# Down projection: the even rows of the raw weights and the rows of x are issued behind the odd rows of the fourth tile

## The chip, the cores and the metric

The kernel runs on one core of a Trainium2 chip. The metric is the device time of one execution in microseconds, the median of three runs: 2437.94 (2428.3 to 2442.87). The profile is of one further execution, which took 2436.62 with a span of 2434.6.

## The reference, cut to what matters

The reference is an encoder of two post-norm layers over a sequence of 1024 rows of 1024 float32 values. Each layer has a token mixer (a convolution group, a differential attention group and an attention over 256 memory rows) and then a channel mixer:

```python
for l in range(DEPTH):
    mixed = hybrid_mixer(x, mem, bias_off, ...)
    x = layer_norm(ALPHA * x + mixed, ln1_g[l], ln1_b[l])
    ff = jnp.square(jax.nn.relu(x @ w_up[l])) @ w_down[l]
    x = layer_norm(ALPHA * x + ff, ln2_g[l], ln2_b[l])
```

`w_up` is 1024 x 4096, `w_down` is 4096 x 1024. The change lies in the product with `w_down`, once in each layer.

## The kernel before

A float32 product is made of three products of halves: every operand is split into a high part, rounded to the matmul's type, and the low part that is left (`split`, lines 96 to 102: ScalarE writes the high part, VectorE the low one). On top of that both products of the channel mixer use a seven-product scheme for 2 x 2 blocks (Strassen's, in Winograd's form): seven block products in place of eight, on sums and differences of blocks.

The up projection goes over 16 pairs of hidden tiles. For each pair it writes seven forms of the hidden values to DRAM (`hd`, `keep`, line 928), since the down projection wants them as its stationary operands.

The down projection (lines 997 to 1152) has two groups `gr` of weight rows, and in each the seven products in the order `PRODS = (3, 1, 5, 6, 2, 7, 4)`. One product is 96 matmuls of 512 columns: four tiles `q`, four row blocks `t`, six matmuls each (two halves of the contraction by three products of halves). A tile `q` of the raw weights, `wd`, is 128 x 4 x 1024: four row groups of 512 KB, each its own DMA from SyncE's queue (`down_raw`, line 1020). `place` (line 1003) says which block a product takes. Product 3, the first, takes block (1, 1), which lies in the odd row groups 1 and 3. Product 1, the second, takes block (0, 0), which lies in the even row groups 0 and 2. From product 5 on the blocks are differences that VectorE makes in place (lines 1034 to 1039), and they need both.

`down_forms` (lines 1028 to 1053) makes one tile's operands for one product: the differences, the split weights `wf` (128 x 1024), the load of the hidden forms `hr` (two DMAs of 256 KB from `hd`, lines 1049 and 1050) and their split `hf`. The raw tiles of the first group lie in slots of the pool tag `b16`, which hold the transposed x of the up projection until its last readers are done. The fourth tile, `wd_0_3`, gets the slot whose last reader is the last matmul group of the up projection (`uc`, line 905).

What sets the order: the Tile framework schedules each engine's instructions from a model of times and allocates the slots. `tc.issue_after(ins)` adds the condition that what the block issues on the engine of `ins` stands behind `ins`. In the kernel before, the even rows of the four tiles and the rows of x for the first four blocks (`yd`, `down_rows`, line 1058) stand behind `loads[-1]`, which is there the last load of hidden forms for product 3, tile 3. That load is early on SyncE's queue, since its pairs are done early.

In names as the instruction order prints them, `wd_0_3` is group 0, tile 3; `wf_0_1_2` and `hf_0_1_2` are group 0, product 1, tile 2; the last number is a buffer's. The profile leaves numbers out: `db` and `dz` are the accumulators of the down projection (`db` of product 3, `dz` of product 1 in the first group).

Of the kernel before, what the change touches and what calls it, by code (L numbers as in the profile page):

```python
# [54 lines left out]
def encoder(ctx: ExitStack, tc: tile.TileContext, x, memt, w_f, w_v, w_mk, w_mv, w_out, w_up,  # L55
# [40 lines left out]
    def split(hi, lo, src, lo_eng=None, hi_eng=None):  # L96

        if hi_eng is None:
            nc.scalar.activation(hi, src, AF.Copy)  # L99
        else:  # L100
            hi_eng.tensor_scalar(hi, src, 1.0, 0.0, ALU.mult, ALU.add)
        (lo_eng or nc.vector).tensor_tensor(lo, src, f(hi), op=ALU.subtract)  # L102

    loads = []
# [661 lines left out]
    for l in range(L):  # L766
# [230 lines left out]
        with ExitStack() as es:  # L997
# [12 lines left out]
            def down_raw(gr, q, rows=(0, 1, 2, 3)):  # L1010

                if (gr, q) not in wr:
                    if gr and q < 2:
                        r = pd.tile([P, 4, 1024], F32, tag="wd", name=f"wd{l}_{gr}_{q}", bufs=2)
                    else:
                        r = big.tile([P, 4, 1024], F32, tag="b16", name=f"wd{l}_{gr}_{q}", bufs=4)
                    wr[gr, q] = r.rearrange("p (b i) (j d) -> p b i j d", b=2, j=2)
                m0 = 4 * (NQ * gr + q)
                for i in rows:
                    loads.append(nc.sync.dma_start(wr[gr, q][:, i // 2, i % 2].rearrange("p j d -> p (j d)"), w_down[l, (m0 + i) * P:(m0 + i + 1) * P, :]))  # L1020

            def form_tile(tag, name, q):

                if q == 3:
                    return wts.tile([P, 2, 2, 512], F32R, tag="w8", name=name, bufs=3)
                return pd.tile([P, 2, 2, 512], F32R, tag=tag, name=name, bufs=3)

            def down_forms(gr, i, q):

                r = wr[gr, q]  # L1030
                v = {k: r[:, :, k[0], k[1]] for k in ((0, 0), (0, 1), (1, 0), (1, 1))}
                tt = nc.vector.tensor_tensor
                if i == 5:
                    tt(v[0, 0], v[0, 1], v[0, 0], op=ALU.subtract)
                    tt(v[0, 1], v[1, 1], v[0, 1], op=ALU.subtract)
                elif i == 6:
                    tt(v[1, 1], v[1, 1], v[0, 0], op=ALU.subtract)
                elif i == 4:
                    tt(v[1, 0], v[1, 1], v[1, 0], op=ALU.subtract)
                if not gr and i == PRODS[0] and q < 2:  # L1040

                    w = [big.tile([P, 2, 512], F32R, tag="y4", name=f"wf{l}_{gr}_{i}_{q}_{n}", bufs=8) for n in range(2)]
                else:
                    w = form_tile("wf", f"wf{l}_{gr}_{i}_{q}", q)
                    w = [w[:, 0], w[:, 1]]
                split(w[0], w[1], v[place[i]])
                hr = wts.tile([P, 2, 512], F32, tag="raw", name=f"hr{l}_{gr}_{i}_{q}", bufs=3)
                p0 = 2 * (NQ * gr + q)
                for n in range(2):
                    loads.append(nc.sync.dma_start(hr[:, n], hd[p0 + n][:, form_of[i]]))  # L1050
                h = form_tile("hf", f"hf{l}_{gr}_{i}_{q}", 3 if not gr and i == PRODS[0] and q < 2 else q)
                split(h[:, 0], h[:, 1], hr)
                return w, h

            def down_rows(ts):
                for t in ts:
                    ys[t] = ytile(f"yd{l}_{t}")
                    nc.sync.dma_start(ys[t], xmid[l][t])
# [44 lines left out]
            cur = []  # L1103
            for q in range(NQ):
                down_raw(0, q, (1, 3))
                cur.append(down_forms(0, PRODS[0], q))

            with tc.issue_after(loads[-1].ins):
                for q in range(NQ):
                    down_raw(0, q, (0, 2))  # L1110
                down_rows(range(4))
# [113 lines left out]
def build(arrays):  # L1225
    import concourse.bacc as bacc

    nc = bacc.Bacc("TRN2", target_bir_lowering=False, num_devices=1, dynamic_dma_scratch_size=1024)
    args = [nc.dram_tensor(f"in_{k}", v.shape, mybir.dt.from_np(v.dtype), kind="ExternalInput").ap() for k, v in arrays.items()]
    args.append(nc.dram_tensor("out_0", (T, D), F32, kind="ExternalOutput").ap())  # L1230
    with tile.TileContext(nc, schedule_with_timeline_sim=True) as tc:
        encoder(tc, *args)
    return nc
# [9 lines left out]
```

## Time and profile before

| | before |
|---|---|
| median of 3 runs | 2437.94 us (2428.3 to 2442.87) |
| profiled execution | 2436.62 us, span 2434.6 us |
| TensorE busy | 2322.3 us (95%), 11516 matmuls |
| VectorE busy | 1770.3 us (73%) |
| ScalarE busy | 1176.0 us (48%) |
| SyncE's DMA queue | 353.81 MB, 43.1% of 16 engines |

The span starts with the first instruction of the program. The chain that ended last lies on TensorE for 77% of the span, so a stretch in which TensorE stands still is where time can go or come from. The shares of the DMA queue are means over stages: in some stretches the queue is full all the time, in others nearly empty, so a stretch has to be read by itself. The first layer's down projection begins at about 912 us, the second's at about 2097 us.

### The profile page before, as it was taken

The numbers are of one execution on the slowest core, as the hardware profiler recorded it, in microseconds if no ns is written. First come the engines' busy times: TensorE is split into PE (matmuls) and PEld (weight loads), VectorE is DVE, ScalarE is ACT, GpSimd is POOL, SyncE is SP. The second block draws the span as 40 slices with busy tenths as digits, with TensorE's granted clock in tenths as the row PEclk, the third lists the DMA queues.
The fourth block names the chain that finished last, engine by engine and source line by source line (L and its number), as shares of the span: only waits on it lengthen the run. The fifth ranks groups of instructions, "written<-read, shape, count | busy, mean of one in ns | idle before, by whom it ended". The sixth has DMA issues, their size and how long they took to land.

```text
span 2434.6 us, 30636 instructions
## 1 busy us (share of the span) xinstructions
PE 2322.3 (95%) x11516; PEld 1944.3 (80%) x11516; DVE 1770.3 (73%) x2516; ACT 1176.0 (48%) x2034; POOL 274.0 (11%) x184
## 2 busy tenths in 40 slices
PE   6999999999999998999999999999999999899997
PEld 5888788787788886888878877887878888688886
DVE  8697868857766657667779967786676666576768
ACT  6212488844655544333431227885465555433332
POOL 2134021110000000000123411112100000000002
PEclk8999999999999999999999999999999999999999
DMA  8252555252344468343322436334324444954332
GB/s 338 88 174 87 184 139 129 72 182 84 125 150 153 150 223 333 98 164 96 114 108 95 130 96 201 90 101 153 110 94 141 161 144 159 348 174 168 97 95 95
DMA packets 137740, 355.76 MB, mean 146 GB/s; under 512 B 14804, under 2 KB 31956, under 8 KB 130900
## 3 DMA queue, kind: packets, MB, share of 16 engines
q1 hardware_dynamic: 137592, 353.81, 43.1%
q8 instruction: 90, 1.47, 0.3%
q14 instruction: 58, 0.48, 0.1%
HBM read 240.47 MB, written 117.47 MB: 147 GB/s over the span
## 4 chain that ended last, share of the span: by engine, by line
PE 77%; DVE 17%; ACT 3%; issue 2%; DMA 2%; SPq 0%; DVEq 0%; ACTq 0%
PE uz L905 14%; PE db L1092 14%; PE dz L1092 10%; PE uc L905 7%; DVE acc L342 7%; PE ud L905 4%; PE wo_ps L117 2%; PE wo_ps L116 2%; PE wo_ps L115 2%; DVE s L536 2%; PE at L187 2%; PE pj L115 2%; PE pj L116 2%; PE pj L117 2%; PE sc L533 1%
## 5 line engine op out<-in xcount | busy, mean ns | idle before, releaser
L1092 PE MATMUL db<-wf,hf 128*128 128x512 f32 x1536 | 359.3, 394 | 19.6 <-ACT hf L99 14.0
L1092 PEld LDWEIGHTS db<-wf,hf 128*128 128x128 f32 x1536 | 291.1, 190 | 83.0 <-ACT hf L99 14.9
L1092 PE MATMUL dz<-wf,hf 128*128 128x512 f32 x1152 | 263.1, 389 | 0.0
L102 DVE TENSOR_TENSOR wf<-wd,wf 128x1024 fp32r<-128x1024 f32 x112 | 138.8, 1239 | 156.9 <-ACT wf L99 149.2
L1092 PEld LDWEIGHTS dz<-wf,hf 128*128 128x128 f32 x1152 | 216.2, 188 | 44.9
L99 ACT ACTIVATE wf<-wd 128x1024 fp32r<-128x1024 f32 x112 | 118.1, 1056 | 249.2 <-PE db L1092 128.8
L99 ACT ACTIVATE wu<-wu_r 128x512 fp32r<-128x512 f32 (+1 forms) x192 | 131.6, 705 | 219.0 <-PE uc L905 96.4
L905 PE MATMUL uz<-x,wu 128*128 128x512 f32 x768 | 190.6, 393 | 0.0
L905 PE MATMUL uz<-xt,wu 128*128 128x512 f32 x768 | 185.7, 389 | 1.0 <-ACT wu L99 1.0
L342 DVE SCALAR_TENSOR_TENSOR acc<-u,pp,acc 128x1009 f32<-128x1009 f32 (+14 forms) x120 | 185.8, 1590 | 0.4
L115 PE MATMUL pj<-x_h,wf 128*128 128x512 f32 x448 | 177.1, 396 | 1.7 <-ACT x_h L99 1.7
L116 PE MATMUL pj<-x_l,wf 128*128 128x512 f32 x448 | 177.2, 396 | 1.6 <-DVE l_row L126 1.6
L117 PE MATMUL pj<-x_h,wf 128*128 128x512 f32 x448 | 175.9, 394 | 0.3 <-POOL wf L102 0.3
L102 DVE TENSOR_TENSOR wu<-wu_r,wu 128x512 fp32r<-128x512 f32 (+1 forms) x192 | 146.0, 778 | 36.7 <-ACT wu L99 36.1
L99 ACT ACTIVATE hf<-hr 128x1024 fp32r<-128x1024 f32 x112 | 117.5, 1049 | 110.3 <-PE db L1092 41.1
L536 DVE CUSTOM_DVE_ANT_0 s<-sc,bt 128x1024 f32<-128x1024 f32 x128 | 153.1, 1218 | 24.2 <-PE sc L534 18.6
L905 PEld LDWEIGHTS uz<-x,wu 128*128 128x128 f32 x768 | 145.6, 190 | 30.6 <-ACT p L916 0.2
L905 PEld LDWEIGHTS uz<-xt,wu 128*128 128x128 f32 x768 | 144.0, 188 | 31.5 <-ACT wu L99 1.6
L166 POOL TENSOR_TENSOR yd<-yd,l2g 128x1024 f32<-128x1024 f32 x6 | 17.2, 2868 | 1294.0 <-ACT yd L165 1294.0
L538 ACT ACTIVATE s<-s,ast 128x1024 f32<-128x1024 f32 x128 | 148.5, 1166 | 26.4 <-DVE ast L536 26.1
L922 DVE TENSOR_TENSOR h<-u,uc 128x512 f32<-128x512 f32 x64 | 44.0, 688 | 138.2 <-PE uc L905 117.3
L102 DVE TENSOR_TENSOR hf<-hr,hf 128x1024 fp32r<-128x1024 f32 x112 | 137.1, 1224 | 4.0 <-ACT hf L99 4.0
(259 smaller groups left out, 5089.9 us busy)
## 6 DMA issues: line engine op xcount, KB each, us to landing
hr<-hd SPq DMA_DIRECT2D x224, 256.0 KB, 2.9
wu_r<-in_w_up SPq DMA_DIRECT2D x64, 512.0 KB, 4.1
hd<-hs SPq DMA_DIRECT2D x128, 256.0 KB, 2.9
wd<-in_w_down SPq DMA_DIRECT2D x64, 512.0 KB, 7.3
hd<-h SPq DMA_DIRECT2D x96, 256.0 KB, 2.1
ks<-kd SPq DMA_DIRECT2D x32, 512.0 KB, 9.8
wf_raw<-in_w_f SPq DMA_DIRECT2D x28, 512.0 KB, 4.5
qd<-stg SPq DMA_DIRECT2D x8, 1024.0 KB, 4.0
```

The lines of the kernel that those rows point to most:

```text
L99: nc.scalar.activation(hi, src, AF.Copy)
L102: (lo_eng or nc.vector).tensor_tensor(lo, src, f(hi), op=ALU.subtract)
L115: nc.tensor.matmul(ps, lhsT=lhs[0], rhs=rhs[0], start=start, stop=False)
L116: nc.tensor.matmul(ps, lhsT=lhs[0], rhs=rhs[1], start=False, stop=False)
L117: nc.tensor.matmul(ps, lhsT=lhs[1], rhs=rhs[0], start=False, stop=stop)
L187: nc.tensor.matmul(pt[:, j * P:(j + 1) * P], lhsT=src, rhs=ident, start=j == 0, stop=j == 3, is_transpose=True, skip_group_check=True)
L342: nc.vector.scalar_tensor_tensor(acc[:, c, a:b], u[:, c, a + t - PAD:b + t - PAD], pp[:, k:k + 1], acc[:, c, a:b], ALU.mult, ALU.add)
L536: nc.vector.tensor_tensor_reduce(out=sc[:, m], in0=ps.rearrange("p a b -> p (a b)"), in1=bt[:, b0:b0 + T], scale=-0.125, scalar=3e38, op0= ...
L538: nc.scalar.activation(sc[:, m], sc[:, m], AF.Exp, scale=-1.0, bias=st[:, m:m + 1], accum_out=st[:, 2 + m:3 + m])
L905: nc.tensor.matmul(ps, lhsT=a[:, kc], rhs=x[:, c, kc], start=start and kc == 0 and n == 0, stop=stop and kc == 3 and n == 2, skip_group_ch ...
L922: nc.vector.tensor_tensor(h, a, ps, op=op)
L1092: nc.tensor.matmul(ps, lhsT=h[:, a, n, ts], rhs=w[c][:, n], start=start and n == 0 and m == 0, stop=stop and n == 1 and m == 2, skip_group ...
```

## The change

`odd` is the last DMA that `down_raw(0, q, (1, 3))` issued. When the loop is done it is the second odd row group of the fourth tile. The even rows and the rows of x now stand behind that DMA in SyncE's queue and no longer behind the last load of hidden forms.

```diff
             for q in range(NQ):
                 down_raw(0, q, (1, 3))
+                odd = loads[-1]
                 cur.append(down_forms(0, PRODS[0], q))
 
-            with tc.issue_after(loads[-1].ins):
+            with tc.issue_after(odd.ins):
                 for q in range(NQ):
                     down_raw(0, q, (0, 2))
                 down_rows(range(4))
```

SyncE's queue in the first layer, where the fourth tile's raw weights are issued. `wd` is raw weights, `yd` rows of x, `hd` stores of hidden forms of the up projection's last pair:

```order
-L1020 DMA wd_0_3_7748<-in_w_down 128x1024 x4
-L1058 DMA yd_3_7774<-xmid_101 128x1024
+L1020 DMA wd_0_3_7748<-in_w_down 128x1024 x2
+L1020 DMA wd_0_0_7710<-in_w_down 128x1024 x2
+L1020 DMA wd_0_1_7723<-in_w_down 128x1024 x2
+L1020 DMA wd_0_2_7736<-in_w_down 128x1024
 L928 DMA hd_15_5187<-hs_15_2_7694 128x512
 L928 DMA hd_15_5187<-hs_15_0_7692 128x512
+L928 DMA hd_15_5187<-hs_15_1_7693 128x512
+L1020 DMA wd_0_2_7736<-in_w_down 128x1024
+L928 DMA hd_15_5187<-hs_15_3_7695 128x512
+L1020 DMA wd_0_3_7748<-in_w_down 128x1024 x2
```

Six even row groups, of tiles 0 to 2, stood ahead of the fourth tile and now stand behind its odd rows; so do the rows `yd_0` to `yd_2`.

The same queue after the change, further on, up to the load of hidden forms for product 1, tile 2:

```order
L1058 DMA yd_3_7774<-xmid_101 128x1024
L1050 DMA hr_0_1_1_7840<-hd_2_5174 128x512
L1050 DMA hr_0_1_1_7840<-hd_3_5175 128x512
L1058 DMA yd_4_7918<-xmid_101 128x1024
L1058 DMA yd_5_7920<-xmid_101 128x1024
L1058 DMA yd_6_7922<-xmid_101 128x1024
L1058 DMA yd_7_7924<-xmid_101 128x1024
L1020 DMA wd_1_0_8074<-in_w_down 128x1024 x4
L1020 DMA wd_1_1_8079<-in_w_down 128x1024 x4
L1050 DMA hr_0_1_2_7873<-hd_4_5176 128x512
L1050 DMA hr_0_1_2_7873<-hd_5_5177 128x512
```

The load `hr_0_1_2` stands behind all of that, as it did before behind the eight rows of `wd_1`.

ScalarE's order in the same place, high parts of the split operands:

```order
 L99 ACTIVATE wf_0_3_3_7751<-wd_0_3_7748 128x1024
 L99 ACTIVATE hf_0_3_3_7757<-hr_0_3_3_7754 128x1024
-L99 ACTIVATE wf_0_1_3_7907<-wd_0_3_7748 128x1024
 L99 ACTIVATE wf_0_3_2_7739<-wd_0_2_7736 128x1024
 L99 ACTIVATE hf_0_3_2_7745<-hr_0_3_2_7742 128x1024
```

The activation `wf_0_1_3`, which reads even rows of the fourth tile, no longer stands between the operands of product 3's tiles 3 and 2; on VectorE its low part and the three differences of `wd_0_3` leave the same place. The second layer's order changes in the same way.

## Rows read from the trace of the kernel before

**Rows 1.** Timeline of TensorE, first layer: start, length, line, count, [idle before <-releaser].

```profile
934.86 2.08 PE L1092 MATMUL db<-wf,hf 128*128 128x512 f32 x4 [6.38 <-ACT hf L99]
939.14 12.38 PE L1092 MATMUL db<-wf,hf 128*128 128x512 f32 x44 [2.20 <-DVE wf L102]
951.35 21.92 PE L1092 MATMUL dz<-wf,hf 128*128 128x512 f32 x96
```

**Rows 2.** Chain that ended last, first layer: start, length, what.

```profile
924.40 7.39 DMA wd<-in_w_down
...
931.86 1.06 ACT wf L99
...
934.21 1.24 DVE wd L1034
...
937.87 1.23 DVE wf L102
```

**Rows 3.** Stretches: length, busy time of each engine, PEclk, DMA share, GB/s.

```profile
905.00:923.00 18.00, 18.00 (x81) 14.93 (x80) 6.94 (x10) 7.99 (x13) 0.00 (x0) 1.00 1.03 414
```

**Rows 4.** Stretches at the granted clock of 0.50, both layers.

```profile
933.42:943.66 10.24, 6.60 (x15) 4.73 (x16) 10.14 (x10) 5.29 (x6) 0.00 (x0) 0.50 1.04 417
...
2117.85:2128.09 10.24, 5.15 (x11) 3.64 (x12) 9.17 (x8) 5.96 (x7) 0.00 (x0) 0.50 1.02 407
```

**Rows 5.** SyncE's DMA issues, timeline of the first layer.

```profile
923.07 1.76 SPq L1020 DMA_DIRECT2D wd<-in_w_down  x4
...
938.37 4.01 SPq L1020 DMA_DIRECT2D wd<-in_w_down  x8
```

**Rows 6.** Tile hr, 943.3 to 945.1 us: issues, first and last start, landing.

```profile
L1050 SPq DMA_DIRECT2D hr<-hd x2: 327/327/327, 943.4 to 944.6; - x2
...
DMA to landing us min/median/max: 8.8/9.1/9.4
```

**Rows 7.** Tile hd, 919.6 to 920.6 us, the last issues ahead of the fourth tile.

```profile
L928 SPq DMA_DIRECT2D hd<-h x2: 320/322/325, 919.7 to 920.2; - x2
...
DMA to landing us min/median/max: 5.1/5.1/5.2
```

**Rows 8.** Tile wd, 893.1 to 894.95 us: four rows into an empty queue.

```profile
L1020 SPq DMA_DIRECT2D wd<-in_w_down x4: 333/422/430, 893.2 to 894.5; - x4
...
DMA to landing us min/median/max: 3.7/6.1/8.1
```

**Rows 9.** Timeline of ScalarE, first layer.

```profile
928.72 1.06 ACT L99 ACTIVATE wf<-wd 128x1024 fp32r<-128x1024 f32 x1 [3.62 <-DMA wd<-in_w_down]
```

**Rows 10.** Timeline of TensorE, second layer.

```profile
2120.73 2.07 PE L1092 MATMUL db<-wf,hf 128*128 128x512 f32 x4 [7.63 <-ACT hf L99]
2125.01 11.70 PE L1092 MATMUL db<-wf,hf 128*128 128x512 f32 x44 [2.21 <-DVE wf L102]
2136.55 21.92 PE L1092 MATMUL dz<-wf,hf 128*128 128x512 f32 x96
```

**Rows 11.** SyncE's DMA issues, second layer.

```profile
2107.69 1.76 SPq L1020 DMA_DIRECT2D wd<-in_w_down  x4
```

**Rows 12.** Tile hr, 2128.9 to 2130.7 us.

```profile
L1050 SPq DMA_DIRECT2D hr<-hd x2: 326/326/326, 2129.1 to 2130.2; - x2
...
DMA to landing us min/median/max: 9.0/9.3/9.5
```

**Rows 13.** Tile hd, 2104.2 to 2105.5 us.

```profile
L928 SPq DMA_DIRECT2D hd<-h x2: 319/319/319, 2104.3 to 2105.0; - x2
...
DMA to landing us min/median/max: 6.3/6.3/6.4
```

**Rows 14.** Timeline of VectorE, first layer: a difference and an accumulation.

```profile
945.81 1.22 DVE L1035 TENSOR_TENSOR wd<-wd 128x1024 f32<-128x1024 f32 x1
946.95 1.22 DVE L1034 TENSOR_TENSOR wd<-wd 128x1024 f32<-128x1024 f32 x1
...
953.82 1.28 DVE L1068 SCALAR_TENSOR_TENSOR yd<-yd,db 128x512 f32<-128x512 f32 x2
```

## The prediction

> **What bounds the kernel now.** I read the timeline of TensorE first, around the start of the down projection, because the change touches nothing else. TensorE runs without a break through the end of the up projection and the first half of product 3. Then it stands still for 6.38 us, does four matmuls, stands still for 2.20, and from 939.14 runs to the end of product 3 at 951.35 [rows 1]. The second layer shows the same with 7.63 and 2.21 [rows 10]. From there each layer's down projection has hardly a gap, so a shift of product 1 goes through to the end.
>
> The chain of waits says what ends the pause. The last even row of the fourth tile is issued at 924.40 and lands 7.39 us later; ScalarE's `wf_0_1_3` waits for it, VectorE's low part and three differences of that tile follow, and only then `wf_0_3_2`, which TensorE needs, at 937.87 [rows 2]. None of the work between is needed by product 3. The odd rows, which are, had landed by 928.72 [rows 9].
>
> The stretches come next, for what the pause costs beside itself and for the queue. From 933.42 to 943.66 the granted clock is 0.50, the lower of the two levels, and TensorE is busy for 6.60 of these 10.24 us; in the second layer for 5.15 [rows 4]. And the DMA engines are full: share 1.03 and 414 GB/s already from 905 to 923, 417 afterwards [rows 3, 4]. A row group of 512 KB (524,288 bytes) takes 1.26 us at 417 GB/s. A queue that is full gives nothing for nothing: what is put behind is late by its own length.
>
> **What the change does at the first pause.** Product 3 gets rid of `wf_0_1_3` and its followers. In the first layer the fourth tile can be issued at 923.07 as before, since its slot comes free with a matmul group of the up projection [rows 5]. The queue is then empty. A first row into an empty queue lands after 3.7 us [rows 8], the second 1.26 later: 928.1, hardly sooner than the 928.72 of before. Four activations of 1.06 (weights and hidden forms of tiles 3 and 2) follow without a wait: TensorE starts at 932.3 rather than 934.86. VectorE's four low parts run beside them and end some 2 us later, so the second pause nearly goes. 48 matmuls at 21.92/96 = 0.228 us are 10.96, up to 3.3 more if the low clock still falls into them: product 3 ends at 943 to 947 and not at 951.35. Seen by itself that is 5 to 8 us in each layer.
>
> **What it adds.** By the order of SyncE's queue, six even row groups and three rows of x, all of 512 KB, move from ahead of the fourth tile to behind its odd rows. They were loaded while TensorE was busy with the up projection; now that time of the queue lies idle. 9 x 1.26 = 11.3 us of transfers are put ahead of everything that follows, and there is no free stretch to take them up. What follows is used in this order.
>
> - Even rows of tile 0, for the first quarter of product 1: five rows behind 923.07, landed by about 932.4. Needed at 943. Hidden; without that cover each microsecond would count.
> - Even rows of the fourth tile: twelve row lengths (hidden forms count half), about 941. They hold up ScalarE and VectorE, but the next in their queues, `hf_0_1_1`, has to wait for its own load until about 949 in any case. Product 1 wants it a quarter (5.5 us) after its start, at 949 to 952. At most 1.6 us, and they only shorten the next wait.
> - `hr_0_1_2`, the hidden forms for product 1's third quarter. In the kernel before it landed at 944.6 + 8.8 = 953.4 [rows 6] and TensorE came to it at 951.35 + 10.96 = 962.3: 8.9 us of cover against 11.3 that are added. This one comes out late.
>
> The new landing of `hr_0_1_2` in the first layer: 953.4, plus 11.3, minus the backlog that stood before the fourth tile, plus what the empty queue loses in starting. The backlog ended at 920.2 + 5.2 = 925.4 [rows 7], 2.3 after 923.07. The start is shown by no row with this mix, so it is bounded. A first row into an empty queue lands after 3.7, 2.4 more than its length; the fourth one at 894.5 + 8.1 = 902.6, which is 9.4 after the first issue and 4.4 more than four lengths [rows 8]. From the low end comes off what the queue of before lost as well: twenty row lengths from 925.4 to 952.1 (one length ahead of 953.4) are 26.7 us and not 25.2. So 0.9 to 4.4; I take 3.0, nearer to the 2.4 of a single first row. The landing is 953.4 + 11.3 - 2.3 + 3.0 = 965.4. ScalarE's high part takes 1.06 [rows 9], TensorE starts the third quarter at 966.5. Before: 962.3. That is +4.2.
>
> The second layer: 2130.2 + 9.0 = 2139.2 [rows 12], plus 11.3, minus (2105.0 + 6.3 - 2107.69) = 3.6 [rows 11, 13], plus 3.0, gives 2149.9, and with the activation 2151.0. Before: 2136.55 + 10.96 = 2147.5 [rows 10]. That is +3.5.
>
> The clock: TensorE ends product 1's second quarter at 954 to 958 and stands still until 966.5, 8 to 12 us, as long as the two pauses of before together (8.6). After those the low clock lasted until 943.66, 4.5 us past the last restart at 939.14, which cost 2.3 us of work. Nothing of this length stands elsewhere in the down projection, so I bound it by 0 and by the 3.3 (half of 6.60) that the first layer lost in all, and take 2.3 a layer. What the clock cost before is inside 951.35 and has not to be taken off again.
>
> **The sum.** 4.2 + 3.5 + 2 x 2.3 = 12.3 us. The profiled execution took 2436.62, 1.3 under the median of the runs shown, so 2436.6 + 12.3 = 2449. Bounds of this case: start 0.9 and clock 0 give 2.1 + 1.4 = 3.5 (2440); start 4.4 and clock 3.3 give 5.6 + 4.9 + 6.6 = 17.1 (2454).
>
> The rate of the queue is what the page DMA: Bandwidth & Descriptors of the Trainium skill sets lower: in its section Where 436 GB/s comes from it says that for transfers between HBM and SBUF the HBM side binds, at about 358 GB/s. The trace has 414 to 417 in these stretches. By the page a row would take 1.46 us, the nine 13.2, and the sum would be some 2453; I keep to the rows.
>
> **Rivals.**
> - The hidden forms come in time and the first gain stays. Then product 3 ends at 943 and not 951.35 (8.4) and in the second layer at about 2127.5 and not 2136.55 (9.0): 2419. For it: product 3 really is held by work that it doesn't need [rows 2]. Against it: `hr_0_1_2` would have to land by 954, and 30 row lengths stand between 923.07 and it; in 31 us that is over 500 GB/s, and no stretch shows more than 417.
> - The wait is only moved: the queue starts with a loss of 0.9 and the clock is back at once. 3.5 us more, 2440. For it: every low bound comes from a row. Against it: both layers lost clock after pauses of this length [rows 4].
> - VectorE's order becomes the bound. After `hf_0_1_1` (high part at about 950.1) it has twelve instructions of 1.14 (the distance of two neighbours) and four accumulations of 0.64 up to the low part of `hf_0_1_2` [rows 14]: 16.2 us, 966.3. By the DMA the same is done at 965.4 + 1.06 + 1.22 = 967.7. If VectorE comes to `hf_0_1_1` later than 951.5, each microsecond counts; 954 would cost 2.6 a layer: 2454. ScalarE also has `wf_0_5_0` and `wf_0_5_1` ahead of `hf_0_1_2`, which wait for TensorE's first two quarters; done by about 959, they are hidden by the load.
>
> **How the numbers follow.** The forecast has 0.58, the moved wait 0.22, VectorE 0.13, the gain 0.07. About 0.5% (12 us) is what a measurement of this kernel can tell from no change. The forecast's 12.3 lies on that border, so half of its chance is slower: 0.29 + 0.13 = 0.42. Within: 0.29 + 0.22 = 0.51. Faster: 0.07. The range leaves out the gain and the outer tails: 2435 to 2457; that of the forecast by itself is 2440 to 2454.
>
> **What would show it.** Right: the pause ahead of product 3's last two tiles is down to 4 us or less; a new one of 8 to 12 us stands inside product 1, between its second and third quarter, and ends with `hf` on a load of `hr`; after it the clock is low for some microseconds; the DMA share before 923 has fallen to a fraction and from there is full for about 40 us. Wrong: no pause in product 1 (the queue was faster, or `hr_0_1_2` was not behind all that), one that ends with a VectorE low part well after the load has landed, or a first pause as long as before.

## The result: slower by 0.64%

The changed kernel takes 2452.81 us (median of 6 runs, 2445.93 to 2454.53) against 2437.56 for the kernel before in the same comparison (6 runs, 2428.3 to 2442.87): a ratio of 1.0064, with a 95% interval of 1.0048 to 1.0080. The forecast was 2449, the range 2435 to 2457. The profiled execution took 2453.5, with a span of 2451.7.

Two executions are best compared over a stage, since the whole spans also differ in places that the change doesn't touch. The stage here runs from the start of the up projection's last group, `uc` (twelve matmuls, which stand among the first ones of product 3), to the start of product 5. Before, on TensorE's timeline (start, length, line, count):

```profile
920.16 2.88 PE L905 MATMUL uc<-x,wu 128*128 128x512 f32 x12
...
973.11 17.16 PE L1092 MATMUL db<-wf,hf 128*128 128x512 f32 x75
...
2104.78 2.88 PE L905 MATMUL uc<-x,wu 128*128 128x512 f32 x12
...
2158.31 21.92 PE L1092 MATMUL db<-wf,hf 128*128 128x512 f32 x96
```

After, the same view, which answers to [rows 1] and [rows 10]; the idle time and what ended it stand in brackets:

```profile
923.24 2.88 PE L905 MATMUL uc<-x,wu 128*128 128x512 f32 x12
...
935.04 13.91 PE L1092 MATMUL db<-wf,hf 128*128 128x512 f32 x48 [3.49 <-ACT hf L99]
948.79 6.07 PE L1092 MATMUL dz<-wf,hf 128*128 128x512 f32 x26
955.30 5.28 PE L1092 MATMUL dz<-wf,hf 128*128 128x512 f32 x22 [0.45 <-DVE hf L102]
970.08 13.48 PE L1092 MATMUL dz<-wf,hf 128*128 128x512 f32 x48 [9.49 <-ACT hf L99]
983.39 6.96 PE L1092 MATMUL db<-wf,hf 128*128 128x512 f32 x30
...
2115.22 2.88 PE L905 MATMUL uc<-x,wu 128*128 128x512 f32 x12
...
2126.86 11.21 PE L1092 MATMUL db<-wf,hf 128*128 128x512 f32 x48 [3.32 <-ACT hf L99]
2137.91 5.60 PE L1092 MATMUL dz<-wf,hf 128*128 128x512 f32 x24
2145.33 1.74 PE L1092 MATMUL dz<-wf,hf 128*128 128x512 f32 x4 [1.82 <-ACT hf L99]
2147.88 7.01 PE L1092 MATMUL dz<-wf,hf 128*128 128x512 f32 x20 [0.81 <-DVE hf L102]
2161.71 13.30 PE L1092 MATMUL dz<-wf,hf 128*128 128x512 f32 x48 [6.81 <-ACT hf L99]
2174.84 10.36 PE L1092 MATMUL db<-wf,hf 128*128 128x512 f32 x45
```

The stage was 52.95 and 53.53 us long and is now 60.15 and 59.62: 13.3 us more in the two layers. The pause ahead of product 3's last tiles has shrunk from 6.38 + 2.20 to 3.49, and from 7.63 + 2.21 to 3.32. A pause of 9.49 (6.81) has come up in the middle of product 1, 48 matmuls in, which is the start of its third quarter.

Of the 17.1 us by which the spans differ, 3.08 lie ahead of the stage (923.24 against 920.16), where the change has nothing. They come from the start of the program, where the granted clock was lower in this execution: from 53 to 70 us its mean was 0.70, and 0.90 in the kernel before. That leaves 0.7 elsewhere.

The chain of waits after (start, length, what) shows what ends the new pause:

```profile
941.96 9.34 DMA yd<-xmid
...
951.32 8.77 DMA wd<-in_w_down
...
960.11 8.77 DMA hr<-hd
...
968.97 1.06 ACT hf L99
...
970.08 13.48 PE dz L1092 x48
```

It is the load `hr_0_1_2`, at the end of a row of transfers that are each issued as an earlier one lands. In this part of the chain no engine stands for more than one activation: the pause is a queue.

Stretches after (start:end, length, busy time of PE, PEld, DVE, ACT and POOL, PEclk, DMA share, GB/s), to be read beside [rows 3] and [rows 4]:

```profile
908.00:926.00 18.00, 18.00 (x81) 14.88 (x81) 7.02 (x10) 7.98 (x13) 0.00 (x0) 1.00 0.57 221
934.01:940.84 6.83, 5.80 (x14) 4.54 (x15) 2.81 (x3) 0.98 (x2) 0.00 (x0) 0.50 1.00 336
964.73:974.97 10.24, 4.89 (x12) 3.88 (x13) 6.71 (x6) 3.28 (x4) 0.00 (x0) 0.50 0.92 350
926.00:969.00 43.00, 30.65 (x121) 24.10 (x119) 33.25 (x33) 13.23 (x15) 0.00 (x0) 0.87 0.99 386
2145.74:2152.57 6.83, 6.02 (x15) 4.24 (x14) 6.83 (x9) 0.48 (x1) 0.00 (x0) 0.50 1.02 419
2159.40:2166.22 6.82, 4.51 (x11) 3.59 (x12) 2.40 (x3) 2.88 (x3) 0.00 (x0) 0.50 0.90 339
```

Before the fourth tile is issued the queue moves 221 GB/s, where it moved 414; from there its engines are busy for 43 us (share 0.99), at a mean of 386 GB/s. What was left undone in the first stretch is what is late in the second. The granted clock is at its lower level around the first layer's restart of product 3 (from 934.01), after both new pauses (from 964.73 and 2159.40) and around the short pauses of the second layer's second quarter (from 2145.74). Around the second layer's restart of product 3 at 2126.86 it is not.

### The profile page after: what moved, and what is told of

Read it like the earlier page. It is cut to its first block, busy times and chain, and to the rows that moved or that the text cites. A ratio compares the mean times of both kernels' runs of the same rounds, so it can differ in the third digit from the quotient of the medians.

```text
span 2451.7 us, 30644 instructions
## 1 busy us (share of the span) xinstructions
PE 2327.1 (95%) x11516; PEld 1945.2 (79%) x11516; DVE 1772.0 (72%) x2516; ACT 1175.2 (48%) x2034; POOL 273.9 (11%) x184
## 4 chain that ended last, share of the span: by engine, by line
PE 74%; DVE 17%; DMA 4%; ACT 3%; issue 2%; SPq 0%; DVEq 0%; ACTq 0%
PE uz L905 14%; PE db L1092 12%; PE dz L1092 10%; PE uc L905 7%; DVE acc L342 7%; PE ud L905 4%; PE wo_ps L117 2%; PE wo_ps L116 2%; PE wo_ps L115 2%; DVE s L536 2%; PE at L187 2%; PE pj L115 2%; PE pj L116 2%; PE pj L117 2%; PE sc L533 1%
## 5 line engine op out<-in xcount | busy, mean ns | idle before, releaser
L1092 PE MATMUL dz<-wf,hf 128*128 128x512 f32 x1152 | 271.7, 397 | 19.4 <-ACT hf L99 18.1
```

The costliest lines, as they stand in the source:

```text
L1092: nc.tensor.matmul(ps, lhsT=h[:, a, n, ts], rhs=w[c][:, n], start=start and n == 0 and m == 0, stop=stop and n == 1 and m == 2, skip_group ...
```

## The experiments

The question is whether the price is the late load by itself, what would be late next without it, and whether the first gain can be had without the price. The changed kernel has the comparison above; the other runs were timed beside the kernel before, the next four of the table beside 35 runs of it (median 2439.15), the last three beside 21 (median 2436.54). The last column is the ratio of each run's time to that of the kernel before, with its 95% interval.

| kernel | stage, layer 1 | layer 2 | sum against before | median against before | ratio, 95% |
|---|---|---|---|---|---|
| before | 52.95 | 53.53 | | | |
| changed | 60.15 | 59.62 | +13.3 | +15.2 | 1.0048 to 1.0080 |
| hidden forms ahead | 52.48 | 51.68 | -2.3 | -0.1 | 0.9984 to 1.0014 |
| even rows only | 56.95 | 55.24 | +5.7 | +2.7 | 1.0001 to 1.0025 |
| rows of x only | 53.28 | 53.22 | 0.0 | -3.1 | 0.9974 to 1.0004 |
| split order only | 48.11 | 48.92 | -9.5 | -9.2 | 0.9950 to 0.9985 |
| control | 53.35 | 53.14 | 0.0 | +0.4 | 0.9983 to 1.0014 |
| even rows only, forms ahead | 47.24 | 47.89 | -11.4 | -12.8 | 0.9919 to 0.9963 |
| split order, forms ahead | 47.70 | 48.33 | -10.5 | -13.1 | 0.9924 to 0.9969 |

The stages are those of one execution, with both layers added up; they and the medians agree within some 3 us everywhere. (In the split order alone, eight matmuls of product 5 stand inside product 1; their 1.81 us are taken off in each layer.)

### The late load put ahead

In the changed kernel, the second group's first rows (`wd_1`, eight rows) and the two constants `l2g` and `l2b` go behind product 1's last load of hidden forms.

```diff
-                    for q in range(2):
-                        down_raw(1, q)
...
+                    with tc.issue_after(p1.ins):
+                        for q in range(2):
+                            down_raw(1, q)
...
                 cur = nxt
+                if n == 0:
+                    p1 = loads[-1]
```

> The changed kernel, with the eight rows of wd_1 and the two rows of the layer norm's constants put behind the hidden forms of product 1's last tile. hr_0_1_2 then stands ten row lengths (12.6 us) nearer to the front, and nothing else of the change is undone. Late hidden forms are the loss: hr_0_1_2 lands by about 956 in the first layer, before TensorE comes to the third quarter (960.6 in the changed kernel's trace), so the pause of 9.49 (second layer 6.81) no longer ends on a load. VectorE is next: its low part of hf_0_1_2 now stands four instructions earlier, at about 963.2 to 964.4, so 3 to 4 us of the first layer's pause stay and under 1 of the second's. 2436 to 2441 if the low clock after the pause goes in part, 2431 if VectorE doesn't matter. If something else than this load holds the third quarter, the pauses stay and the time is 2450 to 2455.

It took 2439.07, as expected; against before that is 15.3 less than the changed kernel. But where the rest goes is only half as I had it. TensorE's timeline of this run:

```profile
939.70 11.21 PE L1092 MATMUL db<-wf,hf 128*128 128x512 f32 x48 [3.31 <-ACT hf L99]
950.75 5.60 PE L1092 MATMUL dz<-wf,hf 128*128 128x512 f32 x24
958.90 9.77 PE L1092 MATMUL dz<-wf,hf 128*128 128x512 f32 x28 [2.55 <-ACT hf L99]
969.36 10.27 PE L1092 MATMUL dz<-wf,hf 128*128 128x512 f32 x44 [0.69 <-DVE hf L102]
980.54 9.63 PE L1092 MATMUL db<-wf,hf 128*128 128x512 f32 x41 [0.91 <-ACT hf L99]
...
2145.38 5.73 PE L1092 MATMUL dz<-wf,hf 128*128 128x512 f32 x24 [1.35 <-DVE hf L102]
2152.85 10.28 PE L1092 MATMUL dz<-wf,hf 128*128 128x512 f32 x44 [1.74 <-DVE hf L102]
2164.23 15.98 PE L1092 MATMUL db<-wf,hf 128*128 128x512 f32 x69 [1.09 <-ACT hf L99]
```

The pauses on `hr_0_1_2` are gone. In their place come smaller ones: `hr_0_1_1`, a quarter earlier, which stands behind the moved rows too (2.55 us, and 28 matmuls that take 9.77 for 6.4, on the lower clock), and VectorE's low parts (0.69, 1.35, 1.74). Two more, of 0.91 and 1.09, stand ahead of product 5 and are this edit's own: `wd_1` now stands ahead of that product's hidden forms, and in the chain of waits the load that ends the first of them is issued at 970.02, as a row of `wd_1` lands (962.44 + 7.56). So the late load was the price of the change. Without it the gain of the first pause is eaten in part by the next two things that the moved rows delay and in part by the new place of `wd_1`. How much each takes was not measured apart: the nine moved rows with `wd_1` still further back were not run.

### The two parts of the move apart

In the changed kernel, the rows of x put back ahead of the fourth tile:

```diff
+            forms_in = loads[-1]
             with tc.issue_after(odd.ins):
                 for q in range(NQ):
                     down_raw(0, q, (0, 2))
+            with tc.issue_after(forms_in.ins):
                 down_rows(range(4))
```

> Only the six even rows move; the rows of x stay behind the old load, ahead of the fourth tile. Nine rows behind become six. If the landing of hr_0_1_2 sets the loss, it lands 3 x 1.25 = 3.8 us earlier in each layer, the pause in product 1 is 5.7 and 3.0 in place of 9.49 and 6.81, and the time is 7.5 under the changed kernel's: about 2445. If VectorE's order sets it (in the changed kernel it stood idle for only 0.9 and 1.9 before the low part of hf_0_1_2), the pause shrinks less, VectorE has no idle time left before that low part, and the time is 2447 to 2450. If the price is that of the idle queue as such and not of the number of rows: 2452.

And the reverse, the even rows put back:

```diff
-            with tc.issue_after(odd.ins):
+            with tc.issue_after(loads[-1].ins):
                 for q in range(NQ):
                     down_raw(0, q, (0, 2))
+            with tc.issue_after(odd.ins):
                 down_rows(range(4))
```

> The kernel before with only the rows of x (yd_0 to yd_3) put behind the fourth tile's last row; the even rows stay where they were. Three rows more stand ahead of hr_0_1_2, at most 3.8 us, and it had 8.9 us of cover: nothing is late. The first pause can only shrink, since the fourth tile finds a shorter queue (its odd rows up to 1.3 us earlier). 2434 to 2438. If every row that is put behind costs its length, cover or not, 2445.

With the even rows alone it is 2441.88, with the rows of x alone 2436.08. The second is as expected: three rows stay within the cover and cost nothing. The first lies 3 us under my 2445; by the stage it is 7.6 us under the changed kernel, against 7.5 expected. The pauses of the run with the even rows:

```profile
967.46 13.80 PE L1092 MATMUL dz<-wf,hf 128*128 128x512 f32 x48 [6.32 <-ACT hf L99]
...
2158.04 12.49 PE L1092 MATMUL dz<-wf,hf 128*128 128x512 f32 x48 [7.42 <-ACT hf L99]
```

Both still end on the load: ScalarE waited 9.51 us on it in the first layer and 10.60 in the second. In the first layer VectorE stood idle for 1.05 ahead of its low part, so there it isn't VectorE's order. In the second it came to the low part without idle time, just as the high part was done, and that layer doesn't tell the two apart. The pauses are longer than the 5.7 and 3.0 that I had expected, though the load lands 3.5 and 3.6 us earlier (3.8 expected). In the second layer this is because TensorE comes to the third quarter sooner: the short pauses and the low clock of product 1's second quarter are gone (48 matmuls in 11.04, in the changed kernel 14.35 from 2137.91 without the two pauses). That gains no time, since the load sets the restart.

The four kernels make a scale. The landing of `hr_0_1_2` after the start of `uc`, first layer, is 33.18 us with no row moved, 38.06 with three, 42.13 with six, 45.64 with nine. ScalarE takes it up at once, with the rows of x alone (`uc` at 919.22) and with the even rows alone (924.14):

```profile
957.39 1.06 ACT L99 ACTIVATE hf<-hr 128x1024 fp32r<-128x1024 f32 x1 [9.40 <-DMA hr<-hd]
966.35 1.06 ACT L99 ACTIVATE hf<-hr 128x1024 fp32r<-128x1024 f32 x1 [9.51 <-DMA hr<-hd]
```

From three to nine rows that is 1.26 us a row in the mean (4.07 for the first three of these, 3.51 for the next), 415 GB/s: about the rate of [rows 4]. To the first step, 4.88 for three rows, 1.1 is added once.

### The first gain without the move

In the kernel before, `made` keeps both instructions of each `split` of hidden forms, and product 1's tile 3 is put behind those of product 3's tile 2 on their engines:

```diff
...
-                split(h[:, 0], h[:, 1], hr)
+                made[gr, i, q] = split(h[:, 0], h[:, 1], hr)
...
-                    nxt.append(down_forms(*steps[n + 1], q))
+                    with ExitStack() as behind:
+                        if n == 0 and q == 3:
+                            for p in made[0, PRODS[0], 2]:
+                                behind.enter_context(tc.issue_after(p.ins))
+                        nxt.append(down_forms(*steps[n + 1], q))
```

> The kernel before with its queue as it was; on ScalarE and VectorE the split weights wf_0_1_3 and the differences of the fourth tile stand behind the operands of product 3's third tile. It takes the first gain of the change without its price. TensorE starts at about 932.5 in place of 934.86, the second pause of 2.2 goes, product 3 ends some 5 us earlier in the first layer and 6 to 9 in the second; hr_0_1_2 lands at 953.4 as before, early enough for a third quarter at about 957. 2424 to 2430. If the instructions that now come later on VectorE hold product 1 instead, the gain is given back there: 2434 to 2440.

It took 2429.94, at the upper end of what was expected, and is faster than before by 0.15 to 0.50%. The queue's order is as it was; only ScalarE's and VectorE's order is the changed kernel's at the place that held product 3. TensorE's timeline:

```profile
939.24 12.79 PE L1092 MATMUL db<-wf,hf 128*128 128x512 f32 x48 [4.04 <-ACT hf L99]
...
964.88 5.74 PE L1092 MATMUL dz<-wf,hf 128*128 128x512 f32 x24 [1.07 <-DVE hf L102]
...
2146.55 5.73 PE L1092 MATMUL dz<-wf,hf 128*128 128x512 f32 x24 [1.79 <-DVE hf L102]
```

The first pause is 0.6 to 0.8 us longer than in the changed kernel, and the third quarter waits little, now for VectorE.

### A control, and both ways with the forms ahead

The second group's rows and the constants go behind product 5's last load, which `p5` keeps at the end of step 1:

```diff
-                    for q in range(2):
-                        down_raw(1, q)
...
+                    with tc.issue_after(p5.ins):
+                        for q in range(2):
+                            down_raw(1, q)
...
                 cur = nxt
+                if n == 1:
+                    p5 = loads[-1]
```

This edit was made on the kernel before, on the run with the even rows only, and on the run with the split order.

> Control: the kernel before with the eight rows of wd_1 and the two rows of constants put behind the hidden forms of product 5, nothing else changed. hr_0_1_2 then lands some 12 us earlier. In the kernel before it was not late (8.9 us of cover), so nothing can be gained: 2436 to 2441. If wd_1's place in the queue had a price or a use of its own (contention with the loads that TensorE waits for, a later lack of wd_1), the time would move by 4 us or more to either side.

> The run with only the even rows moved, and wd_1 with the constants behind the hidden forms of product 5. Of the changed kernel the shorter first pause stays, and the two things that held product 1 in the earlier runs go: hr_0_1_2 lands 12 us earlier than in the run with the even rows only (there 966.3, TensorE came at 961), and VectorE's low part of it stands five instructions earlier than in the run with the hidden forms ahead. The pauses of 6.3 and 7.4 go, and 1 to 3 us of low clock in each layer: 13.7 to 18 us under 2441.9, so 2424 to 2428. If VectorE, whose work for product 1 begins late since the last stores of the up projection stand behind the moved rows, still holds the third quarter, 3 us a layer stay: 2430 to 2434.

> The run with only the split order changed, and wd_1 with the constants behind the hidden forms of product 5. There the pauses ahead of product 1's third quarter are 1.07 and 1.79, ended by VectorE's low part of hf_0_1_2; its load landed 2 us before. Here this low part stands eight instructions earlier: both pauses go, 3 us: 2425 to 2429. If those low parts only push back the differences for product 5 on a VectorE that is busy without a break, a pause of the same length shows before product 5 and the time stays at 2430.

The control stays where it was (2436.90, ratio 0.9999): moving `wd_1` gains nothing where `hr_0_1_2` isn't late. The two others take 2423.72 and 2423.44, both just below what was expected and the fastest of all. On the run with the even rows the edit takes off 15.5 us, each against before. On the split order it takes off 3.9 us by the medians and 1.0 by the stage, and the intervals of the two runs overlap: a gain there is not shown by the times, only that the pauses of 1.07 and 1.79 are gone. With the even rows only:

```profile
942.19 13.96 PE L1092 MATMUL db<-wf,hf 128*128 128x512 f32 x48 [3.36 <-ACT hf L99]
955.99 21.92 PE L1092 MATMUL dz<-wf,hf 128*128 128x512 f32 x96
...
2120.39 13.66 PE L1092 MATMUL db<-wf,hf 128*128 128x512 f32 x48 [3.46 <-ACT hf L99]
2133.89 11.72 PE L1092 MATMUL dz<-wf,hf 128*128 128x512 f32 x51
2146.17 10.50 PE L1092 MATMUL dz<-wf,hf 128*128 128x512 f32 x45 [0.56 <-DVE hf L102]
```

With the split order:

```profile
940.96 12.61 PE L1092 MATMUL db<-wf,hf 128*128 128x512 f32 x48 [5.16 <-ACT hf L99]
953.41 21.92 PE L1092 MATMUL dz<-wf,hf 128*128 128x512 f32 x96
...
2119.73 13.66 PE L1092 MATMUL db<-wf,hf 128*128 128x512 f32 x48 [4.75 <-ACT hf L99]
2133.22 21.92 PE L1092 MATMUL dz<-wf,hf 128*128 128x512 f32 x96
```

Product 1 runs without a break, or with one of 0.56. What remains is the first pause and its low clock (12.61 to 13.96 us for 48 matmuls, 11.21 at the upper level). The two ways are the same within their intervals.

## Why the prediction was right

To compare with the numbers of the prediction, 3.08 us are taken off times of the first layer after, and 10.44 off those of the second (the starts of `uc`).

- The first pause. TensorE restarts at 931.96 (forecast 932.3), the second pause is gone, product 3 ends at 945.7 (943 to 947). The lower clock fell into it after all, from 934.01 to 940.84, which is why it isn't nearer to 943. In the second layer it did not, and product 3 ended at 2127.5.
- The load. `hr_0_1_2` lands at 965.8 (forecast 965.4) and in the second layer at 2150.1 (2149.9). The landing is 12.5 later than before; 11.3 of it are the nine rows, 2.3 of backlog come off, and 3.5 are left over, which the forecast put at 3.0 (between 0.9 and 4.4), as the loss of the empty queue's start. In the second layer it is 3.2 (10.9 = 11.3 - 3.6 + 3.2). The 3.0 was a choice between two bounds, so that it came this close is in part luck. By the scale, what is left over is paid with the first three rows and not again with the six after.
- The third quarter starts 4.7 and 3.8 later than before (forecast 4.2 and 3.5). The pause ahead of it is 9.49 in the first layer but 6.81 in the second, where 8 to 12 were named as the sign: there the second quarter waited 1.82 + 0.81, where at most 1.6 had been allowed, and its clock was low. As the prediction says of these waits, they only shorten the next one, and the load sets the restart.
- The clock: 4.89 and 4.51 us at the lower level after the restarts, 2.4 and 2.3 us of work (forecast 2.3 each). 48 matmuls took 13.48 and 13.30 in place of 10.96.
- The sum: 4.7 + 3.8 + 2.4 + 2.3 = 13.2, forecast 12.3; the stages have 13.3. The medians differ by 15.2. The 2 us between lie within the interval of the ratio (11.7 to 19.5 us), and nothing in the traces was found for them.
- The chances. The prediction took 12 us for the border between slower and no change and gave no change the larger chance, 0.51. The 15.2 lie past that border, so what came out had 0.42. The interval is some 4 us to either side, so the twelve runs tell much less than 12 us apart.
- Smaller readings. The even rows of tile 0 are the third and fourth row of the empty queue, and not the fifth; they had landed by about 931.6 (932.4 in the forecast). The fourth tile's even rows were taken up at 943.3 and not at 941. Neither held TensorE up in the first layer.

What is left over in the load's landing is not the start alone. These are stretches after, in the first layer:

```profile
926.00:928.00 2.00, 2.00 (x11) 1.65 (x9) 0.69 (x1) 1.09 (x2) 0.00 (x0) 1.00 0.28 68
...
934.00:936.00 2.00, 0.96 (x2) 0.83 (x3) 2.00 (x3) 0.99 (x2) 0.00 (x0) 0.50 1.12 301
936.00:938.00 2.00, 2.00 (x6) 1.55 (x5) 0.82 (x1) 0.00 (x0) 0.00 (x0) 0.50 0.81 262
```

The queue loses time twice: an estimated 1.7 us in the first stretch and 1.3 in the two others, reckoned at 415 GB/s. In the second layer the same places have 94, and 299 and 298 GB/s. In the second place the up projection's last stores are under way between the rows; that they are the reason was not tested. The 3.5 is a difference from the kernel before, whose queue dipped too (285 GB/s from 930 to 932), so the two figures need not add up to it.

Of the rivals, the gain without a price would have needed the load by 954. The wait that is only moved (2440) fell with the clock, which came back late in both layers, and with the 3.5 and 3.2 where it had 0.9. VectorE as the bound was close, as these rows of VectorE after show:

```profile
967.90 1.22 DVE L102 TENSOR_TENSOR wf<-wd,wf 128x1024 fp32r<-128x1024 f32 x1
970.05 1.23 DVE L102 TENSOR_TENSOR hf<-hr,hf 128x1024 fp32r<-128x1024 f32 x1 [0.93 <-ACT hf L99]
```

It was done with the work ahead at 969.12, 966.0 in the forecast's time, and stood idle for 0.93 (1.85 in the second layer). By VectorE alone its low part would have ended at about 967.2, where the rival had 966.3; with the load it ended at 968.2. The load was last, but by one to two microseconds; the run with the hidden forms ahead shows VectorE take over.

The rate of the queue needs a word, since the sum by the lower rate (2453) came nearer to the median than mine. The Trainium skill's page DMA: Bandwidth & Descriptors, section Where 436 GB/s comes from, has the HBM side bind at about 358 GB/s for transfers between HBM and SBUF, an estimated 1.46 us a row. The scale has 1.26 us a row, and 419 GB/s stand in the stretch from 2145.74: trace and page differ, and the trace decides. By the Trainium skill's page HBM Reference, section Specifications (TRN2), a core that streams alone gets well more than that share, about 425 GB/s. Only one core runs here, and the trace agrees with this by its 415 and 419. That the sum by the lower rate came nearer is chance.

What the prediction did not see stands in one row of ScalarE after:

```profile
942.21 1.06 ACT L99 ACTIVATE wf<-wd 128x1024 fp32r<-128x1024 f32 x1 [7.21 <-DMA hd<-hs]
```

This is the first activation of product 1. It waits for one of the up projection's last stores (`hs`, four of them issued among the moved rows, 11.0 us to landing by their median, 8.4 before). In the kernel before it came without such a wait:

```profile
934.71 1.04 ACT L99 ACTIVATE wf<-wd 128x1024 fp32r<-128x1024 f32 x1
```

Less the 3.08 it is 4.4 us later now, and VectorE stands idle for 6.48 ahead of its low part. Here the late load covered it; I had counted nine moved rows against loads only, and not against stores in the same queue. That VectorE's work for product 1 starts late for this reason fits the small VectorE waits of the later runs, but no run moved these stores by themselves.

## What to carry to other kernels

A transfer that is moved back in a full queue delays what stands behind it by about its own length; the stores behind it landed later as well. So list what stands behind it with the time at which each is used, and look for the first whose cover (the time between its landing and its use) is shorter than the rows that are put ahead (here 8.9 us against 11.3). If work in an engine's order holds a critical instruction, change that order first, and leave the queue busy: here that gave the gain at no price that the runs show. And a transfer with over 100 us of cover, such as `wd_1` (used by the second group, after five more products of 21.9 us), doesn't belong ahead of one with 9; moving it was worth nothing by itself and some 15 us where the load behind it was late.

## What the runs showed of the hardware

- In a full queue of SyncE a row was issued just as one issued about 9 us earlier landed (the chain after: 941.96 + 9.34, 951.32 + 8.77, 960.11 + 8.77). In the scale a load landed 1.26 us later for each 512 KB put ahead of it, in the mean from three rows to nine.
- The first row into a nearly empty queue landed after 3.60 us (issued 926.15), the second 1.26 later. Up to `hr_0_1_2` some 3.5 us are left over beside the rows and the backlog, and not all at the first row: the rate was 68 GB/s from 926 to 928 and dropped once more, to 301 and 262, from 934 to 938.
- TensorE's granted clock was 0.50, the 1.2 GHz level, around a pause of 3.49 us (934.01 to 940.84, restart at 935.04), and the 48 matmuls after it took 13.91; after a pause of 3.32 in the second layer they ran in 11.21, at the upper level. So a pause of this size cost 2.7 us more than its length, or nothing.
